# Attention scores over all 128 rows, with each head's keys in a zero-padded copy

## The chip, the cores and the metric

The kernel runs on one core of a Trainium2 chip. The metric is device time in microseconds (us), lower is better. One execution is one launch of the whole program, from the inputs in HBM to the output in HBM.

## The reference, cut to what matters

Two layers of a decoder trunk run over 256 tokens of width 1024. In each layer a feed-forward half step stands before and after a mixer. The mixer projects the normed tokens to a gate, to the inputs of a state-space scan (SSD) and to q, k and v of 16 heads of 64; scan and attention are joined by one output projection.

```
h = rms_norm(x, mix_norm[i])
z, xbc, dt_raw, q, k, v = split(h @ w_in[i])
y_ssd = ssd_mixer(silu(conv(xbc)), dt_raw, z, ...)
q = rms_norm(q.reshape(b, s, 16, 64), q_norm[i]);  k = rms_norm(k..., k_norm[i])
scores = einsum("qhe,khe->hqk", q, k) / 8          # e = 64 for every head
y_att = softmax over the masked keys, times v      # three dilated branches, merged
x = x + concat([y_ssd, y_att]) @ w_out[i]
```

A score is a sum over the 64 elements of one head.

## The kernel before

**Tiling.** The tokens are two halves of 128. Every large product is three matmuls in float32r (`mm3`, L245 to L247): high by high, high by low, low by high. Weights come once, in half-pieces of 512 KB, by DMAs in SyncE's queue; ScalarE rounds a half-piece (L161) and VectorE takes the remainder (L163). Small products (scan, scores, attention output) are plain float32; the profile shows each of these as two pairs of a weight load and a matmul, so that a count of x64 is 32 products.

**Order.** The program is written as a main line of dense products, and generators that are advanced by `tick()` between groups of them. A planner then orders each engine's instructions by its own model of time, so that single instructions of a generator land inside a group of three. On the chip each engine runs its instructions in that fixed order.

**Mixer.** First z and dt, then eight pieces of xBC (`pc`), then q, k, v for heads 0 to 7 (b = 0), then for heads 8 to 15 (b = 1) (`pq`), then the output projection (`acc`). Under the `pq` products the scan runs: GpSimd makes `rh` and `rl` (L576, L577), TensorE `pseg` (L580, L581), `pcb` (L586), `pst` (L561), `py` (L601), `po` (L606); the scan's result is transposed at L628.

**Attention.** `qk_norm_T` norms q or k of eight heads, transposes the two token halves on TensorE (L679) and writes them with a ScalarE copy (L680) to `qT` or `kT`, [128, 8, 256]: a column of eight holds two heads, the even one on partitions 0 to 63, the odd one on 64 to 127. `head_pair(pr)` takes one such column. For each of its two heads, the rows `o` of `qT` are the stationary operand and the rows `o` of `kT` the moving one: L695 for the second half of the queries against 256 keys, L696 for the first half against 128. Then VectorE adds the mask and takes the maximum (L701), ScalarE the exponential (L704), VectorE divides (L706, L708), TensorE transposes (L715 to L717), ScalarE copies (L719), and TensorE multiplies with v (L725, L726).

**Buffers.** `kT` lies in slot "e1", which held feed-forward weights before and holds weights of the output projection afterwards.

Of the kernel before, what the change touches and what calls it, by code (L numbers as in the profile page):

```python
"""Two layers of a hybrid decoder trunk (macaron SwiGLU, SSD + dilated attention mixer).

Every large product runs as three float32r passes: each operand is split exactly into a
rounded high part and its remainder, and high*high + high*low + low*high is accumulated in
float32.  Tokens are two halves of 128; the weights stream through SBUF once, in pieces
that the host has laid out contiguously in the order of use.
"""
# [7 lines left out]
F32 = mybir.dt.float32  # L15
F32R = mybir.dt.float32r
I32 = mybir.dt.int32
AF = mybir.ActivationFunctionType
# [32 lines left out]
def tile_hybrid_trunk(ctx: ExitStack, tc: tile.TileContext, x, w_ffn_in, w_ffn_down, w_z, w_dtz,  # L51
# [12 lines left out]

    # ---------------------------------------------------------------- constants
    xs = [cst.tile([128, D], F32, name=f"x{t}") for t in range(2)]
# [20 lines left out]

    # ---------------------------------------------------------------- weight stream
    # Pieces [128, n] in the order of use; each is split in two halves of k tiles.  A half
    # (high, low) sits in a slot: five of its own, four that the mixer's tiles use in turn.  # L90
    PIECES = []
# [22 lines left out]
    def behind(engine):  # L114
        """Queue instructions of an engine behind the norm chain that is under way."""
        return tc.issue_after(guard[engine].ins) if engine in guard else nullcontext()
# [89 lines left out]

    # ---------------------------------------------------------------- helpers
    def split(h_out, l_out, src):
# [3 lines left out]
    def rsqrt(v, shape, v2=None):  # L212
        """1/sqrt(v + EPS) on VectorE: seed from the exponent bits, a quadratic in v*y*y, a Newton step."""
        m = sm.tile(shape, F32, tag="rs_m", name="rs_m", bufs=2)
        y = sm.tile(shape, F32, tag="rs_y", name="rs_y", bufs=2)
        a = sm.tile(shape, F32, tag="rs_a", name="rs_a", bufs=2)
        if v2 is None:
            vec.tensor_scalar(m, v, EPS, None, op0=OP.add)
        else:
            vec.scalar_tensor_tensor(m, v, EPS, v2, op0=OP.add, op1=OP.add)  # L220
        vec.tensor_scalar(a.bitcast(I32), m.bitcast(I32), 1, None, op0=OP.logical_shift_right)
        vec.tensor_scalar(y.bitcast(I32), a.bitcast(I32), -1, RSQRT_SEED, op0=OP.mult, op1=OP.add)
        vec.tensor_tensor(a, y, y, op=OP.mult)
        vec.tensor_tensor(a, a, m, op=OP.mult)
        b = sm.tile(shape, F32, tag="rs_b", name="rs_b", bufs=2)
        vec.tensor_scalar(b, a, RSQRT_C[2], RSQRT_C[1], op0=OP.mult, op1=OP.add)
        vec.tensor_tensor(b, b, a, op=OP.mult)
        vec.scalar_tensor_tensor(y, b, RSQRT_C[0], y, op0=OP.add, op1=OP.mult)
        vec.tensor_tensor(a, y, y, op=OP.mult)
        vec.scalar_tensor_tensor(a, a, -0.5, m, op0=OP.mult, op1=OP.mult)  # L230
        vec.scalar_tensor_tensor(y, a, 1.5, y, op0=OP.add, op1=OP.mult)
        return y
# [10 lines left out]
    def mm3(o, ah, al, bh, bl, first, last):  # L243
        """o += a^T b with both operands split."""
        pe.matmul(o, ah, bh, start=first, stop=False)  # L245
        pe.matmul(o, ah, bl, start=False, stop=False)  # L246
        pe.matmul(o, al, bh, start=False, stop=last)  # L247
# [20 lines left out]
    def normed(t, wB, acc=None, scale=None):  # L268
        """RMSNorm of half t, after its residual add from `acc`."""
        xn = wk.tile([128, D], F32, tag="xn", name="xn")  # L270
# [18 lines left out]

    # ---------------------------------------------------------------- dense units  # L290
    def mm_pair(name, n):
        """Two accumulators, each in its own PSUM bank."""
        return [ps.tile([128, 512], F32, tag="mm", name=f"{name}{i}")[:, :n] for i in range(2)]

    def unit_first(n, xT, t, halves, o):
        """o[tok, n] for one half of the tokens; halves of 4 k tiles each, kept."""
        for a, hf in enumerate(halves):
            for k in range(4):
                c = slice(k * n, (k + 1) * n)
                kk = 4 * a + k  # L300
                mm3(o, xT[0][:, kk, tok(t)], xT[1][:, kk, tok(t)], hf[0][:, c], hf[1][:, c],
                    kk == 0, kk == 7)
            if t:
                st.done(hf)
            tick()

    def unit_tok(n, kper, xT, o):
        """o[t][tok, n] for both halves of the tokens; one half-piece = kper k tiles."""
        for a in range(KT // kper):
# [11 lines left out]
    def unit_ch(xT, o):  # L321
        """o[ch, 2, tok]: one piece of 256 weight columns against all tokens."""
        for a in range(2):
# [11 lines left out]
    def project_out(nk, yT, tail, scale, norm, need=None):  # L335
        """x += scale * (y @ W) and, if there is a next norm, the transposed RMSNorm of x.

        The last `tail` k tiles run for half 0 first, so that its norm runs under half 1's products."""
        wB = None
# [43 lines left out]

    # ---------------------------------------------------------------- feed forward
    def ffn(layer, f, xT, xn, norm, tail):
# [47 lines left out]

    # ---------------------------------------------------------------- mixer
    def mixer(layer, xT, xn, norm, tail):
# [5 lines left out]

        # gate z and the step sizes dt
        zv = wk.tile([128, 2, D], F32, tag="e2", name="zv", bufs=1)
# [11 lines left out]
        def step_sizes():  # L455
            """dt = softplus(u) = max(u, 0) + log(1 + e), e = exp(-|u|), by 2 artanh(e / (2 + e))."""
            yield from after(*[f"xbc{j}" for j in range(8)])
# [23 lines left out]
            yield 1  # L481
            # decay from a position to the end of chunk 0, and from the start of chunk 1
            pd = pt.tile(sh, F32, tag="s", name="pd")
# [21 lines left out]

        # causal convolution in channel layout
        bT, cT = [b[:, 0:4, :] for b in xB]
# [3 lines left out]
        def conv(j, p, dst, ev):  # L511
            """Columns of piece j (two channel tiles) in p -> dst [128, 2, 256]."""
            cv = wk.tile([128, 2, 256], F32, tag="t2", name="cv", bufs=5)
# [23 lines left out]
        def group_in(g, cx):  # L537
            """Token layout of the group's inputs, scaled."""
            hs = slice(4 * g, 4 * g + 4)
# [30 lines left out]
        def decay_mask(g, t):  # L570
            """m[s, h, l] = (C_l . B_s) exp(sum of adt over (s, l]) for s <= l."""
            hs = slice(4 * g, 4 * g + 4)
# [83 lines left out]

        # attention
        qT = wk.tile([128, 8, 256], F32, tag="e0", name="qT", bufs=1)
        kT = wk.tile([128, 8, 256], F32, tag="e1", name="kT", bufs=1)
        vt = [wk.tile([128, D], F32, tag="xn", name=f"vt{t}") for t in range(2)]  # L660

        def qk_norm_T(which, b, pp, dst):
            ss = sm.tile([128, 2, 8], F32, tag="qss", name="qss")
# [12 lines left out]
            for t in range(2):  # L676
                p = pt.tile([128, 4, 128], F32, tag="tr", name="tr")
                for i in range(4):
                    pe.transpose(p[:, i, :], qn[t][:, i * 128:(i + 1) * 128], ident)  # L679
                act.activation(dst[:, 4 * b:4 * b + 4, tok(t)], p, AF.Copy, scale=qkw[:, layer, which:which + 1])  # L680
            events.add(f"qk{which}{b}")
# [3 lines left out]
        def head_pair(pr):  # L685
# [6 lines left out]
            for i in range(2):  # L692
                o = slice(64 * i, 64 * i + 64)
                p = pt.tile([128, 384], F32, tag="s", name="psc")
                pe.matmul(p[:, 0:256], qT[o, pr, 128:256], kT[o, pr, :], start=True, stop=True)  # L695
                pe.matmul(p[:, 256:384], qT[o, pr, 0:128], kT[o, pr, 0:128], start=True, stop=True)  # L696
                sc = wk.tile([128, 384], F32, tag="sc", name="sc", bufs=4)
# [40 lines left out]
        for b, which in QKV_ORDER:  # L738
            pp = mm_pair("pq", 512)
            unit_tok(512, 2, xT, pp)  # L740
            if which < 2:
                spawn(qk_norm_T(which, b, pp, (qT, kT)[which]))
            else:
# [6 lines left out]

    # ---------------------------------------------------------------- layers
    wB = norm_weight(0, 0, nc.sync)
# [17 lines left out]
def _pack(w, kper, n):  # L770
    """(..., K, N) -> (..., K/(128*kper), N/n, 128, kper*n), contiguous pieces."""
    import numpy as np
# [71 lines left out]
```

## Time and profile before

| | |
|---|---|
| timed runs | 1276.01, 1280.18, 1280.53 us; median 1280.18 |
| profiled execution | span 1276.9 us from its first to its last instruction; the page gives no time around the span |
| TensorE matmuls (PE) | 1245.6 us busy, 98% of the span |
| TensorE weight loads (PEld) | 1119.5 us, 88% |
| VectorE (DVE) | 796.3 us, 62% |
| ScalarE (ACT) | 635.6 us, 50% |
| GpSimd (POOL) | 73.9 us, 6% |
| chain that ended last | PE 84%, DMA 7%, DVE 6%, ACT 2%, issue 2% |

The busy time of PE holds a modelled end of each matmul, so that rows overlap; what a matmul takes in a stream is the distance from its start to the next one's start.

### The profile page before, as it was taken

What the parts mean: (1) busy time and instruction counts of PE and PEld (TensorE: products, weight loads), DVE (VectorE), ACT (ScalarE), POOL (GpSimd) and SP (SyncE); (2) the same over time, 40 slices, a digit from 0 to 9 for tenths busy, and PEclk for the clock granted to TensorE, in tenths of its full rate; (3) what the DMA queues carried; (4) which work ended last, traced back from release to release, by engine and by line L of the source; (5) the groups of instructions that cost most, each with busy time, mean ns of one, the idle gap of its engine ahead of it and who ended that gap; (6) DMA issues with size and microseconds to landing.
All of it is one profiled execution on the core that took longest, in us unless ns stands there. A gap on an engine that the chain in (4) does not pass through costs nothing.

```text
span 1276.9 us, 20517 instructions
## 1 busy us (share of the span) xinstructions
PE 1245.6 (98%) x8128; PEld 1119.5 (88%) x8128; DVE 796.3 (62%) x1364; ACT 635.6 (50%) x970; POOL 73.9 (6%) x77
## 2 busy tenths in 40 slices
PE   6999999998899999999999999999989999999998
PEld 5999988997777799998899998889867778999987
DVE  5655536888786666654466654478887856655542
ACT  5544435765555555444345543366636554554430
POOL 0000000024300000000000000000342000000000
PEclk9999999999999999999999999999989999999999
DMA  7665554653233546655447654646522324666551
GB/s 247 225 216 184 177 172 135 206 177 114 99 111 120 180 145 222 213 183 181 165 141 231 204 184 148 199 147 200 166 99 95 121 99 166 191 220 197 183 189 45
DMA packets 59424, 213.81 MB, mean 167 GB/s; under 512 B 6848, under 2 KB 7104, under 8 KB 59328
## 3 DMA queue, kind: packets, MB, share of 16 engines
q1 hardware_dynamic: 58176, 208.76, 49.7%
q0 software_dynamic: 1008, 3.67, 0.9%
q8 instruction: 64, 1.05, 0.3%
q14 instruction: 32, 0.26, 0.1%
q10 hardware_dynamic: 144, 0.07, 0.0%
HBM read 211.42 MB, written 1.05 MB: 166 GB/s over the span
## 4 chain that ended last, share of the span: by engine, by line
PE 84%; DMA 7%; DVE 6%; ACT 2%; issue 2%; SPq 0%; ACTq 0%; DVEq 0%
PE acc L245 9%; PE acc L247 8%; PE acc L246 8%; DMA w<-in_w_ffn_in_dram 7%; PE pu L245 5%; PE pu L246 5%; PE pu L247 5%; PE pg L245 5%; PE pg L246 5%; PE pg L247 5%; PE pq L245 3%; PE pq L246 3%; PE pq L247 3%; PE pc L247 2%; PE pc L245 2%; PE pc L246 2%
## 5 line engine op out<-in xcount | busy, mean ns | idle before, releaser
L163 DVE TENSOR_TENSOR wl<-w,wh 128x1024 fp32r<-128x1024 f32 x268 | 330.1, 1232 | 221.8 <-ACT wh L161 215.5
L161 ACT CAST wh<-w 128x1024 fp32r<-128x1024 f32 x268 | 280.7, 1049 | 307.7 <-DMA w<-in_w_ffn_in_dram 84.0
L163 DVE TENSOR_TENSOR we<-w,we 128x1024 fp32r<-128x1024 f32 x124 | 151.3, 1225 | 140.6 <-ACT we L161 139.4
L161 ACT CAST we<-w 128x1024 fp32r<-128x1024 f32 x124 | 129.5, 1050 | 161.5 <-DMA w<-in_w_ffn_in_dram 51.0
L245 PE MATMUL pu<-xTh,wh 128*128 128x256 f32 x360 | 102.3, 284 | 0.5 <-DVE hh L412 0.5
L245 PE MATMUL pg<-xTh,wh 128*128 128x256 f32 x360 | 102.3, 285 | 0.4 <-ACT sg L406 0.4
L246 PE MATMUL pu<-xTl,wh 128*128 128x256 f32 x360 | 102.0, 283 | 0.0
L247 PE MATMUL pu<-xTh,wl 128*128 128x256 f32 x360 | 102.0, 283 | 0.0
L246 PE MATMUL pg<-xTl,wh 128*128 128x256 f32 x360 | 102.0, 283 | 0.0
L247 PE MATMUL pg<-xTh,wl 128*128 128x256 f32 x360 | 102.0, 283 | 0.0
L245 PE MATMUL pq<-wh,xTh 128*128 128x512 f32 x192 | 82.6, 430 | 0.0
L245 PE MATMUL pu<-xTh,we 128*128 128x256 f32 x280 | 79.5, 284 | 0.4 <-DVE hh L412 0.4
L245 PE MATMUL pg<-xTh,we 128*128 128x256 f32 x280 | 79.7, 284 | 0.0
L246 PE MATMUL pu<-xTl,we 128*128 128x256 f32 x280 | 79.4, 283 | 0.0
L247 PE MATMUL pu<-xTh,we 128*128 128x256 f32 x280 | 79.3, 283 | 0.0
L246 PE MATMUL pg<-xTl,we 128*128 128x256 f32 x280 | 79.3, 283 | 0.0
L247 PE MATMUL pg<-xTh,we 128*128 128x256 f32 x280 | 79.3, 283 | 0.0
L247 PE MATMUL pq<-wh,xTl 128*128 128x512 f32 x192 | 78.4, 408 | 0.0
L246 PE MATMUL pq<-wl,xTh 128*128 128x512 f32 x192 | 77.4, 403 | 0.0
L245 PE MATMUL pc<-xTh,wh 128*128 128x256 f32 x256 | 73.0, 285 | 0.0
L247 PE MATMUL pc<-xTh,wl 128*128 128x256 f32 x256 | 72.6, 283 | 0.0
L246 PE MATMUL pc<-xTl,wh 128*128 128x256 f32 x256 | 72.5, 283 | 0.0
(217 smaller groups left out, 3137.3 us busy)
## 6 DMA issues: line engine op xcount, KB each, us to landing
w<-in_w_ffn_in_dram SPq DMA_DIRECT2D x176, 512.0 KB, 4.7
w<-in_w_ffn_down_dram SPq DMA_DIRECT2D x88, 512.0 KB, 4.5
w<-in_w_qkv_dram SPq DMA_DIRECT2D x48, 512.0 KB, 3.8
w<-in_w_xbc_dram SPq DMA_DIRECT2D x32, 512.0 KB, 4.5
w<-in_w_out_dram SPq DMA_DIRECT2D x32, 512.0 KB, 3.8
w<-in_w_z_dram SPq DMA_DIRECT2D x12, 512.0 KB, 4.9
nw<-in_norms_dram POOLq DMA_DIRECT2D x7, 512.0 KB, 4.3
w<-in_w_dtz_dram SPq DMA_DIRECT2D x4, 544.0 KB, 4.7
```

The lines of the kernel that those rows point to most:

```text
L161: act.copy(h, src)
L163: vec.tensor_tensor(l, src, h.bitcast(F32), op=OP.subtract)
L245: pe.matmul(o, ah, bh, start=first, stop=False)
L246: pe.matmul(o, ah, bl, start=False, stop=False)
L247: pe.matmul(o, al, bh, start=False, stop=last)
```

## The change

Keys are kept in `kz`, [128, 4, 2, 256]: four head pairs, and for each two planes. Plane i holds head i's keys on its own 64 partitions and zeros on the other 64. GpSimd writes the zeros once per layer. The ScalarE copy of the keys becomes two copies of 64 partitions, one per plane. A score product then takes all 128 rows of `qT`, which hold both heads, against one plane of `kz`. `kz` has the size of `kT` and its slot, but room for four pairs instead of eight, so that heads 8 to 15 write over heads 0 to 7 (`pr % 4`). `qT` stays as it is. Comments are also dropped from the file.

```diff
-        kT = wk.tile([128, 8, 256], F32, tag="e1", name="kT", bufs=1)
+        kz = wk.tile([128, 4, 2, 256], F32, tag="e1", name="kz", bufs=1)
+        pool.memset(kz[64:128, :, 0, :], 0.0)
+        pool.memset(kz[0:64, :, 1, :], 0.0)
...
-                act.activation(dst[:, 4 * b:4 * b + 4, tok(t)], p, AF.Copy, scale=qkw[:, layer, which:which + 1])
+                w = qkw[:, layer, which:which + 1]
+                if which:
+                    for i in range(2):
+                        o = slice(64 * i, 64 * i + 64)
+                        act.activation(kz[o, :, i, tok(t)], p[o], AF.Copy, scale=w[o])
+                else:
+                    act.activation(qT[:, 4 * b:4 * b + 4, tok(t)], p, AF.Copy, scale=w)
...
-                o = slice(64 * i, 64 * i + 64)
                 p = pt.tile([128, 384], F32, tag="s", name="psc")
-                pe.matmul(p[:, 0:256], qT[o, pr, 128:256], kT[o, pr, :], start=True, stop=True)
-                pe.matmul(p[:, 256:384], qT[o, pr, 0:128], kT[o, pr, 0:128], start=True, stop=True)
+                pe.matmul(p[:, 0:256], qT[:, pr, 128:256], kz[:, pr % 4, i, :], start=True, stop=True)
+                pe.matmul(p[:, 256:384], qT[:, pr, 0:128], kz[:, pr % 4, i, 0:128], start=True, stop=True)
```

## Rows read from the trace of the kernel before

**Rows 1.** The page, part 1: busy us, share of the span, instructions.
```profile
PE 1245.6 (98%) x8128; PEld 1119.5 (88%) x8128; DVE 796.3 (62%) x1364; ACT 635.6 (50%) x970; POOL 73.9 (6%) x77
```
**Rows 2.** Stretches: length, busy us of PE, PEld, DVE, ACT, POOL; clock, DMA, GB/s.
```profile
360.00:380.00 20.00, 19.94 (x108) 14.60 (x106) 17.45 (x59) 12.12 (x30) 1.32 (x2) 1.00 0.30 101
394.00:425.00 31.00, 31.00 (x150) 23.24 (x149) 17.85 (x62) 18.46 (x45) 0.00 (x0) 1.00 0.29 100
```
**Rows 3.** The wider score product: count, duration ns min/median/max, first and last start, form.
```profile
L695 PE MATMUL psc<-kT,qT x64: 375/428/481, 331.6 to 1051.5; 64*128 64x256 f32 x64
```
**Rows 4.** Timeline around one score: start, us, engine, line, form, [idle before].
```profile
331.23 0.40 PE L247 MATMUL pq<-wh,xTl 128*128 128x512 f32 x1
331.56 0.29 PEld L695 LDWEIGHTS psc<-kT,qT 64*128 64x128 f32 x2 [0.36 <-ACT m L583]
331.56 0.70 PE L695 MATMUL psc<-kT,qT 64*128 64x256 f32 x2
332.10 0.38 PE L696 MATMUL psc<-kT,qT 64*128 64x128 f32 x2
332.40 0.19 PEld L245 LDWEIGHTS pq<-wh,xTh 128*128 128x128 f32 x1
332.41 0.50 PE L245 MATMUL pq<-wh,xTh 128*128 128x512 f32 x1
332.74 0.40 PE L246 MATMUL pq<-wl,xTh 128*128 128x512 f32 x1
```
**Rows 5.** Timeline, 128-row float32 products: 128 moving columns (L586), 256 (L561).
```profile
330.31 0.40 PE L581 MATMUL pseg<-rl,low_r 128*128 128x512 f32 x1
330.32 0.42 PEld L586 LDWEIGHTS pcb<-xB,xB 128*128 128x128 f32 x2
330.55 0.38 PE L586 MATMUL pcb<-xB,xB 128*128 128x128 f32 x2
330.69 0.48 PE L245 MATMUL pq<-wh,xTh 128*128 128x512 f32 x1
331.00 0.39 PE L246 MATMUL pq<-wl,xTh 128*128 128x512 f32 x1
...
339.44 0.40 PE L247 MATMUL pq<-wh,xTl 128*128 128x512 f32 x1
339.68 0.59 PE L561 MATMUL pst<-xe,xB 128*128 128x256 f32 x2
339.92 0.58 PE L245 MATMUL pq<-wh,xTh 128*128 128x512 f32 x1
340.34 0.39 PE L246 MATMUL pq<-wl,xTh 128*128 128x512 f32 x1
```
**Rows 6.** Timeline, ACT and PE: the last copies of keys, heads 8 to 15.
```profile
391.77 0.69 ACT L680 ACTIVATE kT<-tr,qkw 128x512 f32<-128x512 f32 x1 [0.55 <-PE tr L679]
392.36 0.57 ACT L745 COPY vt<-pq 128x512 f32<-128x512 f32 x1
392.82 0.70 ACT L680 ACTIVATE kT<-tr,qkw 128x512 f32<-128x512 f32 x1
393.57 0.70 PE L695 MATMUL psc<-kT,qT 64*128 64x256 f32 x2
```
**Rows 7.** Timeline, ACT: the last copy of keys, heads 0 to 7.
```profile
326.08 0.69 ACT L680 ACTIVATE kT<-tr,qkw 128x512 f32<-128x512 f32 x1 [0.59 <-PE tr L679]
```
**Rows 8.** Timeline, POOL: ahead of and in the scan.
```profile
269.51 0.61 POOL L558 TENSOR_TENSOR xdt<-xdt,hpar 128x256 f32<-128x256 f32 x1 [57.17 <-issue]
276.28 2.04 POOL L576 TENSOR_TENSOR rh<-cc,adh 128x512 fp32r<-128x512 f32 x1
289.60 0.61 POOL L558 TENSOR_TENSOR xdt<-xdt,hpar 128x256 f32<-128x256 f32 x1 [7.30 <-DVE xe L554]
```
**Rows 9.** Stretches of 2 us after a wait of PE; columns as in Rows 2.
```profile
320.00:322.00 2.00, 0.07 (x1) 0.07 (x1) 1.94 (x6) 0.00 (x0) 0.84 (x1) 1.00 0.47 127
324.00:326.00 2.00, 2.00 (x10) 1.82 (x9) 1.99 (x4) 0.69 (x1) 1.16 (x1) 0.50 0.02 4
```

More of the change, by code (lines that the diff above doesn't have):

```diff
@@ L658, in mixer, with qk_norm_T @@
         qT = wk.tile([128, 8, 256], F32, tag="e0", name="qT", bufs=1)
-        kT = wk.tile([128, 8, 256], F32, tag="e1", name="kT", bufs=1)
+        kz = wk.tile([128, 4, 2, 256], F32, tag="e1", name="kz", bufs=1)
+        pool.memset(kz[64:128, :, 0, :], 0.0)
+        pool.memset(kz[0:64, :, 1, :], 0.0)
         vt = [wk.tile([128, D], F32, tag="xn", name=f"vt{t}") for t in range(2)]
-        def qk_norm_T(which, b, pp, dst):
+        def qk_norm_T(which, b, pp):
             ss = sm.tile([128, 2, 8], F32, tag="qss", name="qss")
@@ L741, in mixer @@
             if which < 2:
-                spawn(qk_norm_T(which, b, pp, (qT, kT)[which]))
+                spawn(qk_norm_T(which, b, pp))
             else:
```

## The prediction

> **What bounds the kernel now.** I read the busy shares first: TensorE's matmuls fill 98% of the span, and no other engine passes 62% [rows 1]. An average hides stages, so the stretches of the attention came next. In the second half of the `pq` products, where the scores of heads 0 to 7 run, TensorE is busy 19.94 of 20 us; in the last `pq` products and the first `acc` products, with the scores of heads 8 to 15, 31.00 of 31 [rows 2]. VectorE is the next busiest, at 17.45 of 20 and 17.85 of 31. So time that leaves TensorE's stream here leaves the end, as long as the others keep up. A full PE row says nothing of use: rows overlap, and idle array time can sit inside one. So I then read distances between starts, in the timeline around single products.
>
> **What a score costs now.** Each score is two float32 products of 64 rows, L695 against 256 columns and L696 against 128, each as two loads and two matmuls. The row of L695 counts x64 in this form [rows 3], so there are 32 scores (16 heads, 2 layers). Around the first of them the products of 512 columns start 0.23 us apart (331.00 in [rows 5], 331.23 in [rows 4]). From the last dense product ahead of the score (331.23) to the second behind it (332.74) are 1.51 us [rows 4]. Two dense products account for 0.46, so the score takes 1.05 us of TensorE.
>
> Four pieces of this are not arithmetic. The load for L695 starts only at 331.56, 0.33 after the dense product's start rather than beside it: 0.10 more than the usual distance. That load is then exposed ahead of its own matmul. Behind L696 the next load (L245) starts at 332.40, with its matmul at 332.41, and the matmul after that comes 0.33 later instead of 0.23: again a load in the open, about 0.10, behind a gap of the same size. The row names ScalarE's `m` as what ended the wait; whether that made the gap, or the 64 rows did, is the second rival below.
>
> **What it will cost.** The nearest rows are float32 products of 128 rows [rows 5]. L586 (128 columns, the shape that L696 will have) loads at 330.32, beside the dense product that began at 330.31: no gap, no exposed load. From 330.31 to 331.00 are 0.69 us; less two dense products (0.46) that is 0.23. L561 (256 columns, as L695 will have): 340.34 less 339.44 is 0.90, less 0.46 is 0.44. A score of 128 rows is one of each, 0.67. The number of columns is unchanged, the zero rows pass beside the others, and both loads and matmuls keep their count. Saved: 1.05 - 0.67 = 0.38 each, times 32: 12.2 us.
>
> Bounds: if the 256-column product cost no more than the 128-column one, a score would be 0.46 and the saving 32 x 0.59 = 18.9; if the gap were due to waits of the score, not to its rows, the saving would be nothing. I take 12.2 because L561 is the same width and type.
>
> *A rule against the change.* The trace shows a 128-row load running beside a 128-row matmul (330.32 against 330.31, [rows 5]). The Trainium skill, page "TensorE: Matmul & The Clock Gate", Part 3, "The mechanism", says that a weight load runs beside a matmul in flight only where their row groups differ. By that rule full-row products would keep both exposed loads; it is the third rival below. The trace disagrees with it here.
>
> **What is added on ScalarE.** Each copy of keys is 128 partitions by 512 elements and takes 0.69 to 0.70 us [rows 6, 7]; there are four per layer. It becomes two of 64 partitions and the same 512 elements. Half the partitions might halve the time (then nothing is added) or leave it (0.69 more each). I take the latter, since the row's element count per partition stays: 8 x 0.69 = 5.5 us on ScalarE, which is 50% busy.
>
> For heads 0 to 7 the last copy ends at 326.77 [rows 7] and the first score starts at 331.56 [rows 4]: 4.8 us of cover for 1.4. Nothing on the path. For heads 8 to 15 there is no cover. The last copy runs 392.82 to 393.52 and the score starts at 393.57 [rows 6]. Queued behind the first copy on ScalarE are the copy of v (0.57) and the second copy. In the new order the queue would be 391.77 + 2 x 0.69 + 0.57 = 393.72, then the copy for the even head until 394.41, and for the odd head until 395.1. The even head's score would start 0.9 late, or 1.5 if it waits for both. Behind a waiting score stand the remaining `pq` and then the `acc` products, so TensorE stands still. The planner may place the score later by its own reckoning, behind dense products that are ready; then the loss is nothing. Range 0 to 1.5 per layer; I take 0.5, because the present order puts this score, in the middle of a group of three, just where the keys become ready. Two layers: 1.0 us.
>
> **What is added on GpSimd.** Two fills per layer of 64 x 1024 elements. The trace has no fill of that size. Products of two inputs take 0.61 us for 256 elements and 2.04 for 512 [rows 8], so 1024 would take 2.4 to 4.1 at these rates; a fill reads no input, so I let the low end be half of the first, 1.2. I take 2.4, the nearer rate of a simple operation, so 4.9 us per layer, and nothing on the path. The fills depend on no result, GpSimd stands idle for 57 us up to 269.51, and for 7.3 us up to 289.60 [rows 8], which is about where the text puts them. If that cover goes, they delay `rh` and `rl` and all of the scan: the fourth rival.
>
> **Buffers.** `kz` holds four pairs, so keys of heads 8 to 15 must wait for the scores of heads 0 to 7. Those come before the second half of q, k, v in TensorE's order, and the copies wait for transposes behind them (391.77, [rows 6]). Nothing.
>
> **Sum.** 12.2 less 1.0 is 11.2 us. The profiled execution's span of 1276.9 would become 1265.7. The page gives no time around the span; the median of the runs lies 3.3 above it, and I take the same step from the median: 1280.2 - 11.2 = 1269.0.
>
> **The rivals.**
> *Half of it is given back (chance 0.13).* VectorE at 17.45 of 20 us [rows 2] feeds both the weights and the softmax. If scores come sooner and it does not, TensorE waits for it later. Against: the 8 scores of heads 0 to 7 lie between 331.56 [rows 4] and the end of that stretch at 380, so about half of them fall into its 20 us and shorten it by 1.5 (4 x 0.38), to 18.5, and VectorE still fits; in the other stretch it has 13 us to spare. Half of 11.2 is 5.6: 1274.6.
>
> *The gap is the score's wait, not its rows (0.03).* For: the profile writes a releaser at the load [rows 4]. Against: the L586 load, also behind a slot of the same pool, has none [rows 5]. Then only the 1.0 remains: 1281.2.
>
> *Loads stay in the open (0.03).* The gaps go, the two loads of 0.10 stay: 0.20 x 32 = 6.4 is not saved. 12.2 - 6.4 - 1.0 = 4.8: 1275.4. It is the mechanism that the named page's rule would have here. Against: [rows 5].
>
> *Slower: the fills stand ahead of `rh` (0.05).* If the planner puts both fills of a layer into GpSimd's queue between 269.5 and 276.3, each at 4.1 us, `rh` comes 8.2 late, and with it `pseg`, `m` and TensorE's `py`. Two layers: 16.3. Net 16.3 - 11.2 = 5.1 slower: 1285.3. It decides from 2.8 us per fill (11.2 / 4). For: one product of GpSimd at 276.28 already takes 2.04 there [rows 8]. Against: the fills are ready long before.
>
> **Clock.** After a wait of TensorE in the scan (0.07 us of work from 320 to 322) the granted clock falls: 0.50 from 324 to 326 [rows 9], the lower of the two levels (1.2 GHz). Such a stretch takes longer whichever kernel runs, and whether it comes may differ from one execution to the next; the three runs are 4.5 us apart. I allow 4 us to either side for it.
>
> **How the numbers follow.** The forecast has 0.76, and its own terms reach from 1263 (L695 cheaper than L561, no stall, a luckier clock) to 1273. The rivals at 1274.6 and 1275.4 have 0.16 together; the range goes up to 1276 to hold them and leaves out the last 0.08 above and a little below 1263. A measurement tells about 0.5% from no change, so faster means below 1273.8 and slower above 1286.6. Faster: the forecast, and a small part of the half case, 0.78. Slower: the fills with an unlucky clock, and orders of the planner that I can't see, 0.05. Same: the rest, 0.17.
>
> **What would show it.** L695 and L696 in form 128*128, their loads starting beside the matmul ahead, and 0.67 us per score between dense products: right. A load that starts 0.33 after the dense product: the gap is not the rows'. Keys copied in eight pieces of about 0.69 per layer, and in the 393 us region a wait of L695 for `kz`: its length is the stall. Fills before 269 or in 282 to 290: hidden. The prediction is wrong if scores cost 0.67 and the span falls by less than 8 us; then a wait of TensorE behind the scores must have grown by the difference.

## The result and the profile after

The changed kernel takes 1267.45 us (median of four runs, 1266.99 to 1267.79); the kernel before, 1280.14 (four runs, 1276.01 to 1280.53). The ratio is 0.9904, with a 95% interval of 0.9888 to 0.992. Repeated among the experiments, the same kernel stood at 0.992 (0.9903 to 0.9938), a median of 1269.58. So the gain is 10 to 13 us: 0.008 and 0.0096 of 1280 by the ratios, 12.7 by the medians above. The profiled execution has a span of 1266.0 us, 10.9 below the one of before; the prediction had 1265.7.

The page of the changed kernel, part 1 (busy us, share of the span, instructions) answers to [rows 1]:

```profile
PE 1234.3 (97%) x8128; PEld 1118.9 (88%) x8128; DVE 795.0 (63%) x1364; ACT 642.3 (51%) x978; POOL 78.0 (6%) x81
```

TensorE keeps its 8128 matmuls and loads, and loses 11.3 us of busy time. ScalarE has 8 copies more and 6.7 us more, GpSimd four fills more and 4.1 us more. The two stretches that answer to [rows 2], with the same columns:

```profile
360.00:380.00 20.00, 19.94 (x110) 15.27 (x110) 18.77 (x64) 12.91 (x30) 1.32 (x2) 1.00 0.33 111
390.00:420.00 30.00, 29.90 (x157) 24.12 (x156) 17.68 (x62) 20.82 (x50) 0.00 (x0) 1.00 0.30 105
```

TensorE still fills both. VectorE rose to 18.77 of 20 us and keeps up; the first rival of the prediction put its 17.45 us into a stretch shortened to 18.5, which is 18.9 of 20. Next the products into `psc` in the changed kernel: count, duration in ns (minimum, median, maximum), first and last start, form; compare [rows 3].

```profile
L703 PE MATMUL psc<-kz,qT x64: 377/379/483, 332.1 to 1041.5; 128*128 128x256 f32 x64
L704 PE MATMUL psc<-kz,qT x64: 272/275/275, 332.6 to 1041.8; 128*128 128x128 f32 x64
```

All stand in the form of 128 rows. The timeline of the changed kernel around a score that stands alone (start, us, engine, line, operation), against [rows 4]:

```profile
347.04 0.39 PE L247 MATMUL pq<-wh,xTl 128*128 128x512 f32 x1
347.04 0.42 PEld L703 LDWEIGHTS psc<-kz,qT 128*128 128x128 f32 x2
...
347.27 0.59 PE L703 MATMUL psc<-kz,qT 128*128 128x256 f32 x2
...
347.70 0.38 PE L704 MATMUL psc<-kz,qT 128*128 128x128 f32 x2
...
347.84 0.47 PE L245 MATMUL pq<-wh,xTh 128*128 128x512 f32 x1
...
348.15 0.39 PE L246 MATMUL pq<-wl,xTh 128*128 128x512 f32 x1
```

The load for L703 starts with the dense matmul ahead of it (347.04), not 0.33 later. From 347.04 to 348.15 are 1.11 us; less 0.46 for two dense products, the score takes 0.65 where it took 1.05. The load beside a matmul of the same 128 rows also settles the prediction's third rival: the rule that was quoted from the Trainium skill (page "TensorE: Matmul & The Clock Gate", Part 3, "The mechanism") does not hold for this pair.

The copies of keys and the fills in the changed kernel, by the tile `kz` (columns as above):

```profile
L687 ACT ACTIVATE kz<-tr,qkw x16: 682/683/686, 325.9 to 1016.0; 64x512 f32<-64x512 f32 x16
L661 POOL MEMSET kz<- x2: 950/950/950, 202.8 to 830.8; 64x1024 f32 x2
...
```

Half the partitions take 0.68 us, against 0.69 for all [rows 6]: splitting a copy doubles its cost. A fill takes 0.95 us. The changed kernel's GpSimd timeline has them long before the scan:

```profile
202.80 0.95 POOL L661 MEMSET kz<- 64x1024 f32 x1 [182.06 <-PE acc L247]
203.80 0.95 POOL L662 MEMSET kz<- 64x1024 f32 x1
...
268.76 0.61 POOL L558 TENSOR_TENSOR xdt<-xdt,hpar 128x256 f32<-128x256 f32 x1 [57.26 <-DVE xdt L556]
```

They start when the products that read the slot's feed-forward weights are done, and 64 us lie between them and GpSimd's next arithmetic (in between it only issues a DMA). Last, the place where the prediction put a stall, heads 8 to 15, in the changed kernel's timeline (answers to [rows 6]):

```profile
389.67 2.79 ACT L687 ACTIVATE kz<-tr,qkw 64x512 f32<-64x512 f32 x4 [0.54 <-PE tr L682]
...
391.31 0.40 PE L247 MATMUL pq<-wh,xTl 128*128 128x512 f32 x1
...
391.81 0.70 PE L703 MATMUL psc<-kz,qT 128*128 128x256 f32 x2
...
392.57 0.65 PE L703 MATMUL psc<-kz,qT 128*128 128x256 f32 x2
...
393.20 0.48 PE L245 MATMUL acc<-wh,yT 128*128 128x512 f32 x1
...
393.51 0.39 PE L246 MATMUL acc<-wl,yT 128*128 128x512 f32 x1
...
394.45 1.07 ACT L753 COPY vt<-pq 128x512 f32<-128x512 f32 x2
```

The planner moved both copies of v (L753) behind the keys, so the four pieces run back to back. Still the first score waits. The two scores take 393.51 - 391.31 - 0.46 = 1.74 us, 0.44 above 2 x 0.65. In the kernel before, the same two stand on either side of one dense product (the start of the first is in [rows 6]):

```profile
393.17 0.40 PE L246 MATMUL pq<-wl,xTh 128*128 128x512 f32 x1
...
394.42 0.50 PE L247 MATMUL pq<-wh,xTl 128*128 128x512 f32 x1
394.85 0.70 PE L695 MATMUL psc<-kT,qT 64*128 64x256 f32 x2
...
395.70 0.50 PE L245 MATMUL acc<-wh,yT 128*128 128x512 f32 x1
396.04 0.40 PE L246 MATMUL acc<-wl,yT 128*128 128x512 f32 x1
```

They took 396.04 - 393.17 = 2.87 less three dense products (0.69), 2.18 us, 0.08 above 2 x 1.05. So in the changed kernel this place loses 0.36 more per layer than before, in both layers.

### The profile page after: what moved, and what is told of

Same layout as the page of the kernel before. It is cut to its first block, busy times and chain, and to the rows that moved or that the text cites. A ratio compares the mean times of both kernels' runs of the same rounds, so it can differ in the third digit from the quotient of the medians.

```text
span 1266.0 us, 20534 instructions
## 1 busy us (share of the span) xinstructions
PE 1234.3 (97%) x8128; PEld 1118.9 (88%) x8128; DVE 795.0 (63%) x1364; ACT 642.3 (51%) x978; POOL 78.0 (6%) x81
## 3 DMA queue, kind: packets, MB, share of 16 engines
q8 instruction: 64, 1.05, 0.3%
HBM read 211.42 MB, written 1.05 MB: 168 GB/s over the span
## 4 chain that ended last, share of the span: by engine, by line
PE 87%; DVE 6%; DMA 4%; ACT 2%; issue 1%; SPq 0%; ACTq 0%; DVEq 0%
PE acc L245 8%; PE acc L246 8%; PE acc L247 8%; PE pu L245 6%; PE pu L247 6%; PE pu L246 6%; PE pg L245 6%; PE pg L247 6%; PE pg L246 6%; PE pq L245 3%; PE pq L246 3%; PE pq L247 3%; PE pc L247 2%; PE pc L245 2%; PE pc L246 2%; DMA w<-in_w_ffn_in_dram 2%
```

## The experiments

**The theory** was the prediction's: a 64-row product among 128-row ones costs TensorE a gap and an exposed load on the way in and again on the way out, and that is what padding removes. Rivals: the gain comes from the new order that split copies and fills bring about; the price is one per 64-row product, not one per change of form; and, once those were settled, that the better way is to set two heads beside each other. All times are medians; the ratio is to runs of the kernel before on the same chip.

| kernel | us | ratio | 95% interval |
|---|---|---|---|
| rows_only | 1268.32 | 0.9888 | 0.9872 to 0.9905 |
| copies_only | 1281.0 | 0.9992 | 0.9981 to 1.0002 |
| mix64 | 1283.11 | 1.0011 | 0.9997 to 1.0026 |
| pair64 | 1269.28 | 0.9899 | 0.9885 to 0.9913 |
| pair128 | 1270.83 | 0.9915 | 0.9899 to 0.9931 |
| v_full | 1275.1 | 0.9949 | 0.9933 to 0.9966 |
| pair64_tr | 1270.7 | 0.9924 | 0.9906 to 0.9942 |
| pair64_lag | 1270.06 | 0.9922 | 0.9909 to 0.9935 |
| pair64_urg | 1268.06 | 0.991 | 0.9896 to 0.9925 |
| changed kernel again | 1269.58 | 0.992 | 0.9903 to 0.9938 |

**The rows alone.** On the kernel before; the scores take all rows of `qT` and `kT`, so that the separation of the heads is left out. No fills, no split copies.

```diff
-                o = slice(64 * i, 64 * i + 64)
...
-                pe.matmul(p[:, 0:256], qT[o, pr, 128:256], kT[o, pr, :], start=True, stop=True)
-                pe.matmul(p[:, 256:384], qT[o, pr, 0:128], kT[o, pr, 0:128], start=True, stop=True)
+                pe.matmul(p[:, 0:256], qT[:, pr, 128:256], kT[:, pr, :], start=True, stop=True)
+                pe.matmul(p[:, 256:384], qT[:, pr, 0:128], kT[:, pr, 0:128], start=True, stop=True)
```

> The kernel before, with its score products over all 128 rows of qT and kT. It leaves out the separation of the two heads of a pair: each score is the sum over both. Keys are copied as before, and there are no fills. Theory A (a product of 64 rows between products of 128 costs two gaps and two loads in the open, 0.38 us a score): a score takes 0.67 us, loads start beside the product ahead, and the time falls by 32 x 0.38 = 12.2, to 1268. Rival B (the gaps are waits of the score, or the gain came from the planner's other order once the copies were split): 1.05 us a score and 1280. Rival C (only the gaps go, the loads stay in the open): 0.87 a score and 1274.

A score took 0.65 us here too:

```profile
348.98 0.39 PE L247 MATMUL pq<-wh,xTl 128*128 128x512 f32 x1
...
350.09 0.39 PE L246 MATMUL pq<-wl,xTh 128*128 128x512 f32 x1
```

Between these lie the score and one dense product: 1.11 - 0.46. The ratio is 0.9888, level with the changed kernel. The rows are sufficient. The first two scores of heads 8 to 15 take 1.59 here (393.04 to 395.32, less three dense products), 0.29 above 2 x 0.65, although the copies of keys are whole: against the 0.08 of before, 0.21 of the 0.36 come without the splitting.

**The additions alone.** The kernel before with the fills and the split copies; the scores keep 64 rows.

```diff
+        pool.memset(kT[64:128, 0:4, :], 0.0)
+        pool.memset(kT[0:64, 0:4, :], 0.0)
...
-                act.activation(dst[:, 4 * b:4 * b + 4, tok(t)], p, AF.Copy, scale=qkw[:, layer, which:which + 1])
+                w = qkw[:, layer, which:which + 1]
+                if which:
+                    for i in range(2):
+                        o = slice(64 * i, 64 * i + 64)
+                        act.activation(kT[o, 4 * b:4 * b + 4, tok(t)], p[o], AF.Copy, scale=w[o])
+                else:
+                    act.activation(qT[:, 4 * b:4 * b + 4, tok(t)], p, AF.Copy, scale=w)
```

> The kernel before, with two fills of 64 x 1024 on GpSimd into kT ahead of the copies, and each copy of keys made as two of 64 partitions, each into its own half of kT. Scores stay at 64 rows. Theory A: the copies take 0.69 us each and the first scores of heads 8 to 15 come 0.3 to 1.0 us later in each layer, so the time is 1280 to 1282. Rival B (the gain was the planner's other order): 1268 to 1275. If the fills cost anything, they do here: over 1284 by the rival that put them ahead of rh.

0.9992: fills and split copies neither help nor cost anything that can be measured. Its lone scores stand at 1.04 to 1.05 us (349.92 to 351.42 is 1.50, less 0.46). The rival of the new order falls.

**One product back to 64 rows.** The changed kernel, with only the narrow product on 64 rows (L705 here, and L704 is the wide one, as the lines moved by one).

```diff
+                o = slice(64 * i, 64 * i + 64)
...
-                pe.matmul(p[:, 256:384], qT[:, pr, 0:128], kz[:, pr % 4, i, 0:128], start=True, stop=True)
+                pe.matmul(p[:, 256:384], qT[o, pr, 0:128], kz[o, pr % 4, i, 0:128], start=True, stop=True)
```

> The changed kernel with only the narrow product of each score (128 columns) back at 64 rows; the wide one stays at 128. Theory A, the price is paid per change of form and not per product: the block again has one change to 64 rows and one back, so a score is back at 1.05 us and the whole gain of the score products is gone: 12 us over the changed kernel, level with the one before (within 3 us). Rival (the price is paid per product of 64 rows): half of it, 0.86 a score, 6 us over the changed kernel.

The timeline of this kernel around one score:

```profile
350.48 0.39 PE L247 MATMUL pq<-wh,xTl 128*128 128x512 f32 x1
350.49 0.41 PEld L704 LDWEIGHTS psc<-kz,qT 128*128 128x128 f32 x2
...
350.71 0.59 PE L704 MATMUL psc<-kz,qT 128*128 128x256 f32 x2
...
351.23 0.29 PEld L705 LDWEIGHTS psc<-kz,qT 64*128 64x128 f32 x2 [0.33 <-issue]
351.23 0.48 PE L705 MATMUL psc<-kz,qT 64*128 64x128 f32 x2
...
351.65 0.50 PE L245 MATMUL pq<-wh,xTh 128*128 128x512 f32 x1
...
351.99 0.40 PE L246 MATMUL pq<-wl,xTh 128*128 128x512 f32 x1
```

The score is back at 1.51 - 0.46 = 1.05 us, and the kernel at 1.0011: half of the products on 64 rows cost the whole price. The gap has moved to the inner border: the wide product's two passes take 0.43 (L704 to the next start, in the undisturbed block above: 347.27 to 347.70), here its neighbour starts 0.52 later, and its load is in the open. "issue" in the bracket means that nothing in the profile was waited for. So the price is one per change of form, and the gap is not a wait of the score. The Trainium skill, page "TensorEngine Tiling (Array Packing)", "Key Properties", says that changing the tiling mode drains TensorE; these rows agree in that each change costs time, 0.38 to 0.40 us for going in and coming out around a score. That a drain is what takes it, no run shows.

**Two heads side by side, on 64 rows.** The kernel before, with both heads of a pair issued together, the wide products of both ahead of the narrow ones; the softmax of both follows. No `kz`, fills or split copies.

```diff
+            pps = [pt.tile([128, 384], F32, tag="s", name="psc") for i in range(2)]
             for i in range(2):
                 o = slice(64 * i, 64 * i + 64)
-                p = pt.tile([128, 384], F32, tag="s", name="psc")
-                pe.matmul(p[:, 0:256], qT[o, pr, 128:256], kT[o, pr, :], start=True, stop=True)
-                pe.matmul(p[:, 256:384], qT[o, pr, 0:128], kT[o, pr, 0:128], start=True, stop=True)
+                pe.matmul(pps[i][:, 0:256], qT[o, pr, 128:256], kT[o, pr, :], start=True, stop=True)
+            for i in range(2):
+                o = slice(64 * i, 64 * i + 64)
+                pe.matmul(pps[i][:, 256:384], qT[o, pr, 0:128], kT[o, pr, 0:128], start=True, stop=True)
+            for i in range(2):
+                p = pps[i]
...
-                yield PAIR_LAG[i]
+            yield PAIR_LAG[0] + PAIR_LAG[1]
```

> The kernel before, with the four products of 64 rows of a head pair in one block (even head 256 columns, odd head 256, even 128, odd 128), the softmax of both heads behind it. No fills, no split copies. Theory A with the two heads at work beside each other in the upper and lower rows: a pair costs the 1.05 us that one score costs now, 16 x 1.05 = 16.8 less: 1263, some 4 us faster than the changed kernel. Theory A without overlap: one pair of switches for two heads, 2 x 0.67 + 0.38 = 1.72 a pair, 16 x 0.38 = 6.1 less: 1274. Rival B (waits of the score): each head keeps its own waits, within 2 us of 1280.

This kernel's timeline around a pair:

```profile
333.94 0.40 PE L247 MATMUL pq<-wh,xTl 128*128 128x512 f32 x1
334.27 0.70 PE L695 MATMUL psc<-kT,qT 64*128 64x256 f32 x4
334.81 0.39 PE L698 MATMUL psc<-kT,qT 64*128 64x128 f32 x4
335.12 0.50 PE L245 MATMUL pq<-wh,xTh 128*128 128x512 f32 x1
335.46 0.40 PE L246 MATMUL pq<-wl,xTh 128*128 128x512 f32 x1
```

The counts are x4: two heads, and they take 1.52 - 0.46 = 1.06 us together, as long as one head alone took before (1.05). So the two heads' products ran at the same time. A pair costs 1.06 here against 2 x 0.65 = 1.30 padded, so 16 pairs should be 3.8 us better than the changed kernel. The kernel is only level with it (0.9899). One loss can be seen at the last pair of the layer:

```profile
414.89 0.39 PE L247 MATMUL acc<-wh,yT 128*128 128x512 f32 x1
...
415.21 1.24 PE L695 MATMUL psc<-kT,qT 64*128 64x256 f32 x3
415.49 0.42 DVE L210 TENSOR_TENSOR yT<-po,yT 128x256 fp32r<-128x256 f32 x1
...
415.96 0.18 PEld L695 LDWEIGHTS psc<-kT,qT 64*128 64x128 f32 x1 [0.46 <-DVE yT L210]
...
417.15 0.39 PE L246 MATMUL acc<-wl,yT 128*128 128x512 f32 x1
```

The odd head's second load waits until VectorE has emptied a PSUM buffer of the same pool (L210). The pair takes 417.15 - 414.89 - 0.46 = 1.80 us, 0.75 more than the others, in both layers. The other loss is in the products with v of the output projection: its four pairs take 5.3 us per layer, against 4.0 in the changed kernel, and the loads of two of them wait 0.55 and 0.66 us for ScalarE's copies of `pT` (at 404.20 and 422.56). The two losses make 2.0 per layer, 3.9 together, as much as the pairs should have won.

**The same regrouping on 128 rows** (pair128: the changed kernel with the loops of pair64, on `qT[:, pr, ...]` and `kz[:, pr % 4, i, ...]`).

> The changed kernel (keys in zero-padded planes) with the same regrouping as the one before: both heads' products in one block. A control for what regrouping alone does. Theory A: full-row products can't run beside each other, a pair takes 2 x 0.67 = 1.34 us, the time is that of the changed kernel, 1267.5, within 2 us for the other order of the softmax. If regrouping itself is worth something (fewer breaks in the dense stream), it shows here: 1263 to 1265.

0.9915, with an interval that overlaps both the changed kernel and pair64: the regrouping alone gives nothing that can be measured. Its scores waited longer for the copies of keys (1.9 us over four loads, against 1.1 over two in the changed kernel).

**Taking away the waits of pair64.** Three variants: pair64_lag advances the odd head's softmax one step later, as in the kernel before; pair64_tr does so too and takes the odd head's PSUM buffer from the pool of the transposes; pair64_urg is pair64_lag with the softmax at a high priority in the planner. The lines are against pair64:

```diff
+            pps = [pt.tile([128, 384], F32, tag=g, name="psc") for g in ("s", "tr")]      # pair64_tr
...
+                yield PAIR_LAG[i]                                   # pair64_tr, pair64_lag, pair64_urg
...
+                with tc.high_priority(offset=URGENT):               # pair64_urg, around the softmax
```

> Products of 64 rows with both heads in one block, as in the regrouped run before, but the odd head's scores take a PSUM buffer from the transposes' pair instead of the scan's, and the softmax of the odd head comes one step after that of the even one, as in the kernel before. In the regrouped run the last pair cost 1.80 us instead of 1.05, its odd head waiting for a PSUM buffer, and the products with v 1.2 us more per layer. Theory: those waits were the buffer's and the softmax order's; without them 16 x 1.05 = 16.8 less than the kernel before, 2 to 4 us faster than the changed kernel. Rival: the buffers of the transposes are as scarce, and the waits move to the transposes: level with the regrouped run.

> Products of 64 rows with both heads of a pair in one block, both from the scan's PSUM buffers, and the softmax of the odd head one step behind the even one's, as in the kernel before. If what kept the regrouped runs at about 12 us instead of 16.8 was the order of ScalarE's work (in the last two pairs of a layer weight casts went ahead of the exponentials, and the products with v waited), this order, nearer to the first kernel's, gives 2 us of it back: 1265 to 1268 by the first kernel's median of 1280 to 1282. Rival: the buffers decide, level with the regrouped run, 1269.

> The same, with the softmax of both heads at a high priority in the planner. Same theory: the exponentials go ahead of the weight casts and the products with v wait less, 1265 to 1267. Rival: the casts that are pushed back delay the weights of the output projection instead: 1270 or more.

None beats the changed kernel: 0.9924, 0.9922, 0.991. What TensorE spends in an output projection beside the dense products (0.229 us each) is 11.6 us in the changed kernel, 12.6 in pair64, 12.0 to 12.2 in pair64_tr, 11.7 in pair64_lag, 12.0 in pair64_urg. No variant took both waits away and kept the pairs whole. In pair64_tr the last pair takes 1.05 us, so that wait was the buffer's; but in each layer the planner set the heads of two of the first four pairs apart (a head alone at 371.97 takes 1.04), and in the output projection the transposes take 4.1 us instead of 3.5 and the products with v 4.8 to 5.0, as its rival had it. In pair64_lag the products with v are back at 4.2, but the last pair takes 1.85, and the first pair of layer 0 takes 2.42 behind a wait. In pair64_urg the last pair takes 1.65 to 1.73 and the products with v 4.7. So pairs set side by side cost less by themselves, and what waits around them take back is as much; whether an order without these waits would beat padding is left open.

**The products with v on the full width.** The same question in columns: in the changed kernel the products with v write 64 columns of the array, one head each (L733, L734). Here each takes all 128 columns of v, so that the separation of the heads in the output is left out.

```diff
-                h, o = 2 * pr + i, slice(64 * i, 64 * i + 64)
-                pe.matmul(po[o, :], vt[0][:, h * E:(h + 1) * E], pTs[i][:, 0:256], start=True, stop=False)
-                pe.matmul(po[o, 128:256], vt[1][:, h * E:(h + 1) * E], pTs[i][:, 256:384], start=False, stop=True)
+                hs = slice(2 * pr * E, 2 * (pr + 1) * E)
+                pe.matmul(po, vt[0][:, hs], pTs[i][:, 0:256], start=i == 0, stop=False)
+                pe.matmul(po[:, 128:256], vt[1][:, hs], pTs[i][:, 256:384], start=False, stop=i == 1)
```

> The changed kernel with the products with v made full as well: both heads' 128 columns of v are the stationary operand of each head's product, and the four products of a pair are summed. It leaves out the separation of the two heads in the output. Theory A, with what the regrouped scores showed (two heads of a pair run beside each other when they stand together): the products with v already stand together and cost about 1.0 us a pair (0.90 in the output stage); full ones can't overlap and cost 2 x 0.65 = 1.30, so this is 16 x 0.3 to 0.4 = 5 to 6 us slower than the changed kernel: 1273. Rival (a change of form always costs more than it saves): 16 x 0.38 = 6 us faster.

Slower than the changed kernel: 0.9949 against 0.9904, which is 0.0045 x 1280 = 5.8 us, or against the 0.992 of its repetition, which is 3.7. First the changed kernel's timeline, then this one's:

```profile
385.24 0.39 PE L247 MATMUL pq<-wh,xTl 128*128 128x512 f32 x1
385.56 0.66 PE L733 MATMUL po<-pT,vt 128*64 128x256 f32 x4
...
386.37 0.50 PE L245 MATMUL pq<-wh,xTh 128*128 128x512 f32 x1
386.71 0.40 PE L246 MATMUL pq<-wl,xTh 128*128 128x512 f32 x1
```

```profile
405.14 0.39 PE L247 MATMUL acc<-wh,yT 128*128 128x512 f32 x1
405.37 0.59 PE L733 MATMUL po<-pT,vt 128*128 128x256 f32 x2
...
406.60 0.48 PE L245 MATMUL acc<-wh,yT 128*128 128x512 f32 x1
406.91 0.40 PE L246 MATMUL acc<-wl,yT 128*128 128x512 f32 x1
```

The narrow form pays the same gap (0.32 from 385.24 to 385.56), but both heads run beside each other: 1.47 - 0.46 = 1.01 us for the pair, against 1.77 - 0.46 = 1.31 for the full form. 16 pairs at 0.30 are 4.8 us; in this execution the last pair of layer 1 also waited 1.3 us for a copy of `pT`. Here padding pays where the narrow products stand apart, as the scores did, each head by itself between dense products, and loses where they stand together.

**The changed kernel again** (after_again), for its spread and clock.

> The changed kernel once more, on the same chip as the two runs beside it, for the comparison with them and for a second profile. Same ratio as before within its interval (0.990), so 1267 to 1269. In the first profile the scores gave back 12.2 us in TensorE's stream; stretches at the lower clock in the scan and short waits for weights in the second feed-forward step of layer 0 (2.4 us) stood on top. If those are chance, they differ in this profile while the score blocks are the same; if the change makes them, they come again at the same places.

0.992. Its trace differs from the first one's in the clock. The stretches of layer 1's scan, first in the changed kernel, then in its repetition (the granted clock is the third number from the end; 1.00 is 2.4 GHz, and a mean below it holds a part at 1.2 GHz, which [rows 9] show behind a wait of TensorE in the scan):

```profile
915.00:940.00 25.00, 21.79 (x114) 17.50 (x113) 20.46 (x37) 11.42 (x21) 9.72 (x9) 1.00 0.34 121
940.00:965.00 25.00, 21.73 (x107) 17.53 (x106) 19.72 (x42) 14.67 (x31) 15.10 (x15) 0.93 0.25 87
```

```profile
915.00:940.00 25.00, 22.30 (x111) 18.36 (x111) 20.02 (x35) 10.79 (x19) 9.56 (x9) 0.93 0.32 111
940.00:965.00 25.00, 21.71 (x101) 17.67 (x100) 18.37 (x42) 13.64 (x30) 13.40 (x15) 0.86 0.23 75
```

The same instructions, and the means lose 0.07 in the one execution and 0.21 in the other (0.07 of 25 us is 1.75 us of full speed). The q, k, v stage of this layer has 48.6 us beside its dense products in the first and 50.6 in the second. So in this layer 2 us came and went with the clock.

## Why the prediction was right, step by step

*What bounds it.* Right: time taken from TensorE's stream left the end. VectorE, nearest to full, kept up, and the giving back of the first rival did not come.

*The price of a score.* Predicted 1.05 to 0.67; measured 1.05 to 0.65 where a score stands alone, 1.05 to 0.72 for the first of a layer (a wait for `m`), 1.23 to 0.98 for one next to another small product (at 360.65). The 256-column product takes 0.43, as the choice of L561 [rows 5] had it. A score right behind six transposes saves as much as a lone one: the run takes 1.70 before and 1.31 after. In the output projections, where no score waits for keys, TensorE spends 13.9 us beside the dense products in the kernel before and 11.6 in the changed one, 0.39 for each of six scores. Of 32 that would be 12.5, where the prediction had 12.2 gross. Added up over all runs of small products that hold a score, TensorE's stream shows 46.7 us in the kernel before and 35.1 in the changed one: 11.7, the stall told below included. Against the additions alone it is 46.2 less 35.1, 11.2: there the first two scores of heads 8 to 15 stand next to each other, with one change of form in and one out for both, and take 1.94 instead of 2.18 in each layer.

*Why it was so dear.* The gap is the form's and not a wait's (second rival): the odd product of mix64 shows it with nothing waited for. The loads went under cover (third rival). Both were argued from two rows; the runs show it.

*The stall of heads 8 to 15* was mis-sized: 0.5 per layer predicted, 0.36 measured, 0.7 for both layers in place of 1.0. That it came near is in part luck: the prediction laid it to the split copies behind a copy of v, but the planner moved the copy of v behind them, and with whole copies rows_only has 0.21 of the 0.36 (0.29 less the 0.08 of before).

*The copies* cost what the whole ones cost (0.68), as taken, and *the fills* 0.95 each, where 2.4 was taken from two-input products, below even the lower end of 1.2. They came 66 us ahead of the earlier of the two places that the prediction named, behind the last reader of the slot, which it had not looked for. The fourth rival falls: no part of the scan stands behind them.

*The sum.* Predicted 11.2. The spans differ by 10.9, the medians by 12.7, the repetition's ratio makes 0.008 x 1280.89 = 10.2. The step from span to median was taken as 3.3 us for both kernels; in the changed kernel it is 1.5 (the profiled execution's own time is 1267.79, 1.8 above its span), since the profile of before was of a quicker execution than the median: at the same 1.8 above its span it took about 1278.7, by estimate. That accounts for the 1.5 us by which the median came out below the forecast. Within the span not all is scores. By distances between the first products of each stage (changed less before), the stages ahead of q, k and v in layer 0 give -0.83, q, k, v and the output projection of layer 0 -4.05, the feed-forward steps and projections between them and q, k, v of layer 1 +1.18, q, k, v and the output projection of layer 1 -6.43, the rest -0.74. The two attention stages thus won 10.5 of the 11.7. The clock is next to the missing part in size: in layer 0's scan the means from 290 to 315 and 315 to 340 us were 1.00 and 0.93 in the profile of before and 0.93 and 0.86 in this one, 0.14 lower in sum; in layer 1 (915 to 965) they were 0.93 and 0.93 before and 1.00 and 0.93 here, 0.07 higher. At the 2 us that went with 0.14 in the repetition, the net 0.07 is 1 us, an estimate; no run isolates it. The +1.18 holds a delay of 2.4 us in a feed-forward step, where two starts of TensorE lie 1.11 and 1.62 us behind the ones ahead of them (from 487.34 and 492.75), with ScalarE waiting for weights close by (1.35 us at 487.07); in the repetition that step took 0.03 more than before, so it is chance. That the span met the forecast within 0.3 us is therefore in part luck: the scores gave 0.5 more than forecast, and clock and weights took as much back.

## What to carry to other kernels

Read the price of a small product from the starts of the dense ones on either side of it: TensorE's busy share reads 98% with the 0.4 us in each score and 97% without. A narrow product among full ones pays on the way in and out, and one narrow product of a score paid here as much as two, so bring one form together: two half-height products of different halves, issued next to each other, cost no more than one, and padding with zeros is the way where they can't be issued together. Once they are, as the products with v here, padding loses. Setting products together also moves the work around them: the paired scores lost their gain again to waits for a buffer and for copies.

## What the runs showed that was not expected

- The price is per change of form: a score with one of two products on 64 rows costs as much (1.05 us) as with both.
- A ScalarE copy from PSUM of 64 partitions by 512 takes 0.68 us, of 128 by 512 0.69.
- A GpSimd fill of 64 x 1024 elements takes 0.95 us, less than twice the 0.61 of a two-input product of 256 elements [rows 8].
